# An MLP's second product on quarters by Strassen's scheme, interleaved with the next group's first product

## The chip, the core and the metric

The kernel runs on one core of one Trainium2 chip. The metric is device microseconds from start to end of one execution; the verdict on a change compares medians of several runs of both kernels.

## What is computed

One layer of a hybrid decoder, for a prompt of 1024 tokens and a sample of 8 x 8 = 64 tokens that share the weights (`D_MODEL` 1024, `D_FF` 4096). After the mixer and its output projection comes the part that the change touches:

```python
    x = x + gate1[:, None] * mixed

    h2 = rms_norm(x, norm2_g[l]) * (1.0 + scale2[:, None]) + shift2[:, None]
    ff = jnp.square(jax.nn.relu(h2 @ w_ff1[l])) @ w_ff2[l]
    x = x + gate2[:, None] * ff
```

The gate is one vector for the whole prompt, and another for each of the eight samples.

## The kernel before

Features lie on the partitions, tokens on the free axis: 1088 tokens in three chunks `CH` of 384, 384 and 320, the last with 256 prompt and the 64 sample tokens. Inputs are fp32. Every operand of a large product is kept as two fp32r parts, `hi` (a rounded copy, made by ACT) and `lo` (the remainder, made by a subtraction on DVE or POOL), and a product is three matmuls: hi x hi, hi x lo, lo x hi (`product`, whose matmuls all stand at line 150 of the profile).

`x1` (128 x 8 x 1088) holds x after the output projection (`out_block`), and `h2` the normed and modulated parts (`make_h2`). The 4096 hidden features go in `NG` = 8 groups of 4 blocks of 128. `ff1(g)` is the first product of a group: for 4 blocks and 3 chunks a product over 8 blocks of `h2` (24 matmuls), then relu (L1270) and square (L1272) on ACT, and DVE squares again in fp32 and subtracts to get the low part (L1273, L1274). `ff2(g)` is the second: for 8 output blocks and 3 chunks a product over the group's 4 blocks (12 matmuls), which DVE multiplies by the gate and adds into `x1` (`add_gated`, L1180 for the prompt, L1183 and L1185 for the sample). `ff1(g + 1)` is issued ahead of `ff2(g)`, so that TensorE always has a whole product between a group's hidden features and their use.

Weights come as 512 KB tiles over SP's queue (two raw tiles `w`), ACT copies `wh` (L229), POOL forms `wl` in the MLP and DVE before it (L230). Products go round four PSUM banks `mm`. TensorE keeps the order in which the code is written; on ACT, DVE, POOL and SP a scheduler sets the order from the dependencies, and each then runs its queue in order. In the last group every output block is stored as it is finished.

## Time and profile before

| | us |
|---|---|
| median of 3 runs (1263.47 to 1264.85) | 1263.8 |
| the profiled execution | 1262.94 |
| its span, first to last instruction | 1261.1 |
| TensorE busy (7836 matmuls) | 1243.6 |
| DVE busy | 657.1 |
| ACT busy | 375.7 |
| POOL busy | 173.6 |

Busy time counts an engine's instructions, not what they achieve: matmuls overlap in TensorE's pipeline, so that one has a length of about 0.33 us while the next starts after 0.15 to 0.17. The distance of starts is what a matmul costs. The granted clock of TensorE was full (2.4 GHz) in 0.999 of the span.

### The profile page before, as it was taken

How to read it: one execution, taken by the hardware profiler on the slowest of the kernel's cores; microseconds unless marked ns; L12 is line 12 of the kernel's file. 1: busy time of each engine (PE TensorE's matmuls, PEld its weight loads, DVE VectorE, ACT ScalarE, POOL GpSimd, SP SyncE). 2: the span in 40 equal slices, each digit the busy share in tenths (PEclk: the TensorE clock that was granted, in tenths of full speed). 3: DMA queues.
4: the chain of work that ended last, by engine and by line, in shares of the span. 5: the costliest groups of instructions: out<-in, count | busy, mean ns of one | idle time of the engine just before them, and what ended most of it. 6: DMA issues, size and time to landing. Idle time of an engine off the chain costs nothing.

```text
span 1261.1 us, 18691 instructions
## 1 busy us (share of the span) xinstructions
PE 1243.6 (99%) x7836; PEld 1194.4 (95%) x7836; DVE 657.1 (52%) x1272; ACT 375.7 (30%) x724; POOL 173.6 (14%) x103
## 2 busy tenths in 40 slices
PE   8899999999999999999999999999999999999998
PEld 6698789998899999999999999999999999999998
DVE  4789798894786539644334334334334334334333
ACT  5372333432465316533023123023023023023000
POOL 3300000000000000022212112112122122122120
PEclk9999999999999999999999999999999999999999
DMA  9548811120122601011111111111111111110122
GB/s 363 187 131 310 219 51 51 51 53 19 35 70 79 197 18 35 1 51 50 35 50 50 34 51 46 39 50 43 42 51 41 45 50 38 46 51 34 50 78 99
DMA packets 41067, 94.42 MB, mean 75 GB/s; under 512 B 11799, under 2 KB 21143, under 8 KB 40983
## 3 DMA queue, kind: packets, MB, share of 16 engines
q1 hardware_dynamic: 40839, 93.16, 23.1%
q8 instruction: 61, 1.00, 0.3%
q14 instruction: 23, 0.19, 0.0%
q10 hardware_dynamic: 144, 0.07, 0.0%
HBM read 86.70 MB, written 6.52 MB: 74 GB/s over the span
## 4 chain that ended last, share of the span: by engine, by line
PE 92%; DVE 4%; DMA 2%; ACT 1%; issue 0%; SPq 0%; DVEq 0%
PE mm L150 85%; PE pm L150 5%; PE pm L154 1%; PE ada L150 1%; DMA ada<-in_ada 1%; DVE ut L279 1%; DMA M<-in_xT 1%; DMA glu<-in_st_conf 0%; DVE lo L286 0%; DVE M L588 0%; DVE lo L283 0%; DVE sq L421 0%; DVE sq L419 0%; DVE uhi L1205 0%; ACT hi L453 0%
## 5 line engine op out<-in xcount | busy, mean ns | idle before, releaser
L150 PE MATMUL mm<-hi,wh 128*128 128x384 f32 (+1 forms) x1208 | 397.9, 329 | 0.1
L150 PE MATMUL mm<-lo,wh 128*128 128x384 f32 (+1 forms) x1208 | 394.4, 327 | 2.1 <-DVE lo L455 2.0
L150 PE MATMUL mm<-hi,wl 128*128 128x384 f32 (+1 forms) x1208 | 394.2, 327 | 0.5 <-DVE wl L230 0.5
L230 POOL TENSOR_TENSOR wl<-w,wh 128x1024 fp32r<-128x1024 f32 x61 | 146.8, 2406 | 843.8 <-ACT wh L229 843.8
L1180 DVE SCALAR_TENSOR_TENSOR x<-mm,mod,x 128x384 f32<-128x384 f32 (+1 forms) x216 | 123.6, 572 | 253.0 <-PE mm L150 244.5
L150 PE MATMUL mm<-uhi,wl 128*128 128x384 f32 (+1 forms) x768 | 251.3, 327 | 0.0
L150 PE MATMUL mm<-ulo,wh 128*128 128x384 f32 (+1 forms) x768 | 250.9, 327 | 0.0
L150 PE MATMUL mm<-uhi,wh 128*128 128x384 f32 (+1 forms) x768 | 250.8, 327 | 0.0
L150 PEld LDWEIGHTS mm<-hi,wh 128*128 128x128 f32 x1208 | 226.9, 188 | 7.7 <-issue 6.0
L150 PEld LDWEIGHTS mm<-lo,wh 128*128 128x128 f32 x1208 | 227.0, 188 | 2.9 <-DVE lo L455 2.9
L150 PEld LDWEIGHTS mm<-hi,wl 128*128 128x128 f32 x1208 | 226.9, 188 | 0.8 <-DVE wl L230 0.8
L1273 DVE TENSOR_TENSOR ut<-ut 128x384 f32<-128x384 f32 (+1 forms) x96 | 95.0, 991 | 237.0 <-ACT uhi L1272 237.0
L229 ACT CAST wh<-w 128x1024 fp32r<-128x1024 f32 x83 | 87.0, 1048 | 433.1 <-PE mm L150 433.1
L150 PEld LDWEIGHTS mm<-uhi,wl 128*128 128x128 f32 x768 | 144.3, 188 | 0.0
L150 PEld LDWEIGHTS mm<-uhi,wh 128*128 128x128 f32 x768 | 144.2, 188 | 0.0
L150 PEld LDWEIGHTS mm<-ulo,wh 128*128 128x128 f32 x768 | 144.2, 188 | 0.0
L588 DVE SCALAR_TENSOR_TENSOR M<-glu,cmix,M 128x512 f32<-128x512 f32 (+2 forms) x150 | 97.9, 668 | 2.0
L1270 ACT ACTIVATE ut<-mm 128x384 f32<-128x384 f32 (+1 forms) x96 | 45.1, 471 | 174.4 <-PE mm L150 174.4
L1274 DVE TENSOR_TENSOR ulo<-ut,uhi 128x384 fp32r<-128x384 f32 (+1 forms) x96 | 51.2, 534 | 3.1
L1272 ACT ACTIVATE uhi<-ut 128x384 fp32r<-128x384 f32 (+1 forms) x96 | 48.7, 509 | 2.9
L150 PE MATMUL mm<-hi,ulo 128*128 128x384 f32 (+1 forms) x144 | 47.0, 326 | 0.0
L150 PE MATMUL mm<-lo,uhi 128*128 128x384 f32 (+1 forms) x144 | 47.0, 326 | 0.0
(229 smaller groups left out, 1125.2 us busy)
## 6 DMA issues: line engine op xcount, KB each, us to landing
w<-in_w_ff SPq DMA_DIRECT2D x64, 512.0 KB, 3.6
w<-in_w_in SPq DMA_DIRECT2D x22, 512.0 KB, 5.1
M<-in_ada SPq DMA_DIRECT2D x20, 512.0 KB, 4.6
ada<-in_ada SPq DMA_DIRECT2D x16, 512.0 KB, 10.2
sw<-in_ada SPq DMA_DIRECT2D x9, 512.0 KB, 5.0
w<-in_w_out SPq DMA_DIRECT2D x8, 512.0 KB, 3.6
out_yT<-x SPq DMA_DIRECT2D x7, 544.0 KB, 2.7
M<-in_xT SPq DMA_DIRECT2D x2, 1536.0 KB, 11.0
```

The source lines that it names most:

```text
L150: return tc.keep_in_program_order(nc.tensor.matmul(*args, **kw))
L154: return tc.keep_in_program_order(nc.tensor.transpose(*args, **kw))
L229: ACT.copy(hi, raw)
L230: lo_engine.tensor_tensor(out=lo, in0=raw, in1=hi, op=ALU.subtract)
L279: DVE.scalar_tensor_tensor(t[:, :w], src[:, :w], a[:, k, 0:1], r[:, :w], ALU.mult, ALU.mult)
L588: DVE.scalar_tensor_tensor(dst, src(t), cdw[:, j, t : t + 1], dst, ALU.mult, ALU.add))))
L1180: DVE.scalar_tensor_tensor(dst[:, :pw], ps[:, :pw], gate[:, 0:1], dst[:, :pw], ALU.mult, ALU.add)
L1270: ACT.activation(t, ps, AF.Relu)
L1272: ACT.activation(uh, t, AF.Square)
L1273: DVE.tensor_tensor(out=t, in0=t, in1=t, op=ALU.mult)
L1274: DVE.tensor_tensor(out=ul, in0=t, in1=uh, op=ALU.subtract)
```

## The change

The seven groups 0 to 6 run their second product by Strassen's scheme in Winograd's form. The group's weights (4 x 8 blocks) and its hidden prompt features (4 blocks x 1024 tokens) are each cut in four quarters: `quarter(g, i, j)` loads a quarter of the weights (i the half of the output features, j the half of the group's hidden blocks) as one 512 KB tile, and `u.quarter(i, j)` is a tile of 128 x 1024 hidden features. In place of eight quarter products there are seven, on quarters or on sums of quarters: DVE adds or subtracts whole fp32 quarters (`s` of weights, `t` of features), `form` has ACT copy the high part (`ah`, `qh`) and DVE subtract the low part (`al`, `ql`), and `products` runs 6 matmuls of 512 columns for each of 4 output blocks. Each result is added into one or two quarters of `x1` (`add_to`), 40 additions in a group.

`x1` therefore holds the sums of the scheme and not x any more: x is stored to a DRAM tensor `x1_save` after the output projection, read back at the end (`xr`), and the gate is applied once, after the last group. The last group runs its eight quarter products straight, on top of the sums.

The 64 sample tokens take no part in the scheme. Their features, high and low part side by side (`st`, 128 columns), are the stationary operand and the unsummed weight quarters the moving one: 4 quarters x 4 matmuls of 512 columns a group, added in `acc`; at the end `pair` adds the two halves (4 fp32 matmuls of 64 columns for each half of the outputs).

The work is written as seven `slot`s a group, with one or two products of the next group's first part between (`ff1_items`, 12 in a group). DVE forms all low parts, POOL has none. ACT and DVE, from group 0's first product on, keep the order in which the code is written (`InOrder`). Hidden features stay fp32 until a slot needs their parts. Seven PSUM banks go round, the eighth is the sample's. The tiles' rooms change with it (`room`), `ut` takes `qh` and `ql` in turn.

```diff
-    ACT, DVE, POOL = nc.scalar, nc.vector, nc.gpsimd
+    POOL = nc.gpsimd
+    pinned = [False]
+    class InOrder:
+        def __init__(self, engine):
+            self.engine = engine
+        def __getattr__(self, name):
+            f = getattr(self.engine, name)
+            if not pinned[0] or name.startswith("dma"):
+                return f
+            def kept(*args, **kw):
+                i = f(*args, **kw)
+                tc.keep_in_program_order(i)
+                return i
+            return kept
+    ACT, DVE = InOrder(nc.scalar), InOrder(nc.vector)
...
+        BUFS = {"ar": 2, "ah": 2, "al": 2, "qh": 2, "ql": 2, "q12": 2}
+        def room(tag, dtype=F32):
+            if tag[0] == "w":
+                return wp.tile([P, 1024], dtype, tag=tag, name=nm(tag), bufs=2)
+            return up.tile([P, 1024], dtype, tag=tag, name=nm(tag), bufs=BUFS.get(tag, 1))
...
-            return up.tile([P, 384], dtype, tag="ut", name=nm("ut"), bufs=5)[:, :w]
+            UT.append(UT.pop(0))
+            return room(UT[-1], dtype)[:, :w]
...
+        def cast(raw, hi, lo):
+            ACT.copy(hi, raw)
+            return lambda: DVE.tensor_tensor(out=lo, in0=raw, in1=hi, op=ALU.subtract)
+        def two(raw, hi_tag, lo_tag):
+            hi, lo = room(hi_tag, F32R), room(lo_tag, F32R)
+            cast(raw, hi, lo)()
+            return hi, lo
...
+        RAW = ("w", "w", "ar", "ar")
+        turn["raw"] = 0
+        def quarter(g, i, j):
+            raw = room(RAW[turn["raw"] % 4])
+            turn["raw"] += 1
+            nc.sync.dma_start(raw.rearrange("p (q f) -> p q f", q=2),
+                              A["w_ff2"][g, 2 * i : 2 * i + 2].rearrange("q p f -> p q f")[:, :, H * j : H * j + H])
+            return raw
+        def block(w, k, m):
+            s = (m // 2) * H + k * 256 + (m % 2) * P
+            return w[:, s : s + P]
+        def products(ps, m, w, u, start, stop):
+            for k in range(2):
+                uh, ul = (x[:, k * H : k * H + H] for x in u)
+                wh, wl = (block(x, k, m) for x in w)
+                PE.matmul(ps, wh, uh, start=start and k == 0, stop=False)
+                PE.matmul(ps, wh, ul, start=False, stop=False)
+                PE.matmul(ps, wl, uh, start=False, stop=stop and k == 1)
...
+        def ff1_split(x, hi="wh", lo="wl"):
+            if x < NG * G:
+                ff1_weights[x] = two(ff1_weights[x], hi, lo)
+        def ff1_block(u, x, c, ps):
+            product(ps, *ff1_weights[x], act_of(h2, c), range(8))
+        def ff1_out(u, x, c, ps):
+            for cols, dst in u.pieces(x % G, c):
+                ACT.activation(dst, ps[:, cols], AF.Relu)
+                ACT.activation(dst, dst, AF.Square)
...
+        save = nc.dram_tensor("x1_save", (P, 8, SEQ), F32, kind="Internal").ap()
+        nc.sync.dma_start(save, x1[:, :, 0:SEQ])
+        pinned[0] = True
+        acc = wide_room("acc")
+        BANKS = [f"mm{x}" for x in range(4)] + [f"pm{x}" for x in range(3)]
+        def next_bank():
+            BANKS.append(BANKS.pop(0))
+            return pp.tile([P, 512], F32, tag=BANKS[-1], name=nm("ps"))
...
+        def form(raw, side):
+            parts = room(side + "h", F32R), room(side + "l", F32R)
+            return parts, cast(raw, *parts)
...
+            if first and g == 0:
+                if minus:
+                    DVE.tensor_scalar_mul(dst, ps, -1.0)
+                else:
+                    DVE.tensor_copy(dst, ps)
+            else:
+                DVE.tensor_tensor(out=dst, in0=dst, in1=ps, op=ALU.subtract if minus else ALU.add)
...
+            st = up.tile([P, G, P], F32R, tag="st", name=nm("st"), bufs=1)
+            ACT.copy(st[:, :, 0:64], u.sample)
+            DVE.tensor_tensor(out=st[:, :, 64:P], in0=u.sample, in1=st[:, :, 0:64], op=ALU.subtract)
+            return st
+        def sample_product(ps, st, w, j, start, stop):
+            for k in range(2):
+                for x in range(2):
+                    PE.matmul(ps.rearrange("p (q m) -> p q m", q=2), st[:, 2 * j + k, :],
+                              w[x].rearrange("p (q k m) -> p q k m", q=2, k=2)[:, :, k, :],
+                              start=start and k == x == 0, stop=stop and k == x == 1)
...
-        def ff2(g, u, last):
-            for mp in range(4):
-                hi, lo = weight_split(*weight(A["w_ff2"][g, mp], POOL))
-                for m2 in range(2):
-                    m = 2 * mp + m2
-                    for c, (c0, w) in enumerate(CH):
-                        ps = mm_psum(w)
-                        product(ps, hi, lo, lambda k: (u[c][0][:, k, :], u[c][1][:, k, :]), range(G),
-                                lambda x: (2 * x + m2) * P)
-                        add_gated(x1[:, m, c0 : c0 + w], ps, c, mod[:, 40 + m, :], ut() if c == 2 else None)
-                        if last and m == 7:
-                            nc.sync.dma_start(O["yT"][:, m, c0 : c0 + w], x1[:, m, c0 : c0 + w])
-                    if last and m < 7:
-                        nc.sync.dma_start(O["yT"][:, m], x1[:, m])
-        u = ff1(0)
-        for g in range(NG):
-            nxt = ff1(g + 1) if g + 1 < NG else None
-            ff2(g, u, g == NG - 1)
-            u = nxt
...
+        def first_parts(g, u, a11):
+            t = room("t")
+            DVE.tensor_tensor(out=t, in0=u.quarter(0, 1), in1=u.quarter(0, 0), op=sub)
+            w, r0 = form(a11, "a")
+            v, r1 = form(u.quarter(0, 0), "q")
+            r0()
+            r1()
+            return t, (w, v)
+        a11 = quarter(0, 0, 0)
+        t, now_parts = first_parts(0, u, a11)
+        s = quarter(0, 1, 0)
+        a22, a12 = quarter(0, 1, 1), quarter(0, 0, 1)
...
+                    ps = next_bank()[:, : CH[c][1]]
+                    ff1_block(nu, x, c, ps)
+                    ff1_out(nu, x, c, ps)
+                    if c == 0:
+                        ff1_split(x + 1)
+                        ff1_load(x + 2)
...
+            def slot(parts, targets, rests):
+                rests = list(rests)
+                for m in range(4):
+                    ps = next_bank()
+                    products(ps, m, *parts, True, True)
+                    if rests:
+                        rests.pop(0)()
+                    for i, j, minus, first in targets:
+                        add_to(g, (i, j, m, minus, first), ps)
...
+            DVE.tensor_tensor(out=s, in0=s, in1=a22, op=add)
+            w, r0 = form(s, "a")
+            v, r1 = form(t, "q")
+            parts2 = (w, v)
+            slot(now_parts, [(0, 0, 0, 1), (1, 1, 0, 1)], [r0, r1])
+            st = sample_parts(g, u)
+            ff1_items(1)
+            sm = sample_bank()
+            sample_product(sm, st, now_parts[0], 0, True, False)
+            ff1_items(1)
+            DVE.tensor_tensor(out=s, in0=s, in1=a11, op=sub)
+            DVE.tensor_tensor(out=t, in0=u.quarter(1, 1), in1=t, op=sub)
+            w, r0 = form(s, "a")
+            v, r1 = form(t, "q")
+            parts3 = (w, v)
...
+            w, r0 = form(a21, "a")
+            slot(parts7, [(1, 0, 0, 0)], [r0])
+            sm = sample_bank()
+            sample_product(sm, st, parts7[0], 1, True, False)
+            sample_product(sm, st, w, 0, False, True)
+            sample_out(g, 1, sm)
+            if not last:
+                a11 = nxt
+                t, now_parts = first_parts(g + 1, nu, a11)
+                a22, a12 = quarter(g + 1, 1, 1), quarter(g + 1, 0, 1)
+            else:
+                weights, parts = {(0, 0): two(nxt, "ah", "al")}, {(0, 0): two(nu.quarter(0, 0), "qh", "ql")}
+            ff1_items(1)
+            u = nu
...
+        weights[0, 1] = two(s, "ah", "al")
+        for ij, tags in (((1, 0), ("qh", "ql")), ((0, 1), ("q12", "t")), ((1, 1), ("fr", "q11"))):
+            parts[ij] = two(u.quarter(*ij), *tags)
+        st = sample_parts(g, u)
+        for j in range(2):
+            weights[1, j] = two(quarter(g, 1, j), "wh", "wl")
+        xr = [hp.tile([P, 4, CH[0][1]], F32, tag=("hi0", "lo0", "hi1", "lo1")[m % 4], name=nm("xr")) for m in range(8)]
+        xr = [x.rearrange("p a b -> p (a b)")[:, 0:SEQ] for x in xr]
+        for m in range(8):
+            nc.sync.dma_start(xr[m], save[:, m, :])
+        s22 = x1[:, 4:8, H:SEQ]
+        for x in (x1[:, 0:4, H:SEQ], x1[:, 4:8, 0:H]):
+            DVE.tensor_tensor(out=x, in0=x, in1=s22, op=ALU.add)
...
+        for i in range(2):
+            sm = sample_bank()
+            for j in range(2):
+                sample_product(sm, st, weights[i, j], j, j == 0, j == 1)
+            sample_out(g, i, sm)
+            for t in range(2):
+                for m in range(4):
+                    ps = next_bank()
+                    for j in range(2):
+                        products(ps, m, weights[i, j], parts[j, t], j == 0, j == 1)
+                    x = x1[:, 4 * i + m, H * t : H * t + H]
+                    gate = mod[:, 40 + 4 * i + m, 0:1]
+                    DVE.scalar_tensor_tensor(x, x, gate, xr[4 * i + m][:, H * t : H * t + H], ALU.mult, ALU.add)
+                    DVE.scalar_tensor_tensor(x, ps, gate, x, ALU.mult, ALU.add)
+                    if t == 0 and m == 1:
+                        sample_end(i)
+                    nc.sync.dma_start(O["yT"][:, 4 * i + m, H * t : H * t + H], x)
```

Where the scheme starts, ACT's queue was, at the end of group 0's first product (`mm` 741 is its last block, 752 the first of group 1):

```order
L1270 ACTIVATE ut_740_5291<-mm_739_5266 128x320 [waits DVE_49,PE_49]
L1272 ACTIVATE uhi2_690_4883<-ut_740_5291 128x320 [waits Activation_49]
L1270 ACTIVATE ut_742_5321<-mm_741_5296 128x320 [waits DVE_49,PE_49]
L1272 ACTIVATE uhi2_690_4883<-ut_742_5321 128x320 [waits Activation_49]
L1270 ACTIVATE ut_753_5363<-mm_752_5338 128x384 [waits DVE_49,PE_49]
L1272 ACTIVATE uhi0_743_5326<-ut_753_5363 128x384 [waits Activation_49]
L1270 ACTIVATE ut_755_5393<-mm_754_5368 128x384 [waits DVE_49,PE_49]
L1272 ACTIVATE uhi1_745_5328<-ut_755_5393 128x384 [waits Activation_49]
L229 CAST wh_768_5526<-w_767_5524 128x1024 [waits DMAHW6_49,PE_49,Pool_49]
```

and is now (`mm` 730 is that last block, `q22` and `us` its prompt and sample part, `w` the quarter (0, 0), `q11` the features' quarter):

```order
L1359 ACTIVATE q22_724_5155<-mm_730_5277 128x256 [waits PE_49]
L1359 ACTIVATE us_727_5214<-mm_730_5277 128x64
L1360 ACTIVATE q22_724_5155<-q22_724_5155 128x256 [waits Activation_49]
L1360 ACTIVATE us_727_5214<-us_727_5214 128x64 [waits Activation_49]
L158 CAST wh_733_5310<-fr_731_5306 128x1024 [waits DMAHW7_49]
L158 CAST ah_738_5320<-w_736_5316 128x1024 [waits DMAHW5_49]
L158 CAST qh_740_5323<-q11_700_4929 128x1024
L158 CAST ah_745_5335<-w_742_5328 128x1024 [waits DMAHW6_49,DVE_49]
L158 CAST qh_747_5338<-t_737_5318 128x1024
```

Before, the next block of the first product followed at once; now the copies of the first quarter stand there.

At a group's end DVE's queue was (group 0's second product: two output blocks of three chunks; nothing else stood between):

```order
L1180 SCALAR_TENSOR_TENSOR x1_3993<-mm_792_5767,mod_76,x1_3993 128x384 [waits PE_49]
L1180 SCALAR_TENSOR_TENSOR x1_3993<-mm_793_5781,mod_76,x1_3993 128x384 [waits PE_49]
L1180 SCALAR_TENSOR_TENSOR x1_3993<-mm_794_5795,mod_76,x1_3993 128x256 [waits PE_49]
L1183 TENSOR_TENSOR ut_795_5808<-mm_794_5795,mod_76 128x64
L1185 TENSOR_TENSOR x1_3993<-ut_795_5808,x1_3993 128x64 [waits DVE_49]
L1180 SCALAR_TENSOR_TENSOR x1_3993<-mm_799_5818,mod_76,x1_3993 128x384 [waits PE_49]
L1180 SCALAR_TENSOR_TENSOR x1_3993<-mm_800_5832,mod_76,x1_3993 128x384 [waits PE_49]
```

and is now, from the last slot of group 1 to the first additions of group 2 (`sm` the sample's product, `t`, `al` and `ql` the next group's first parts, `ar` 920 its `s`, `ps` 945 its first product):

```order
L158 TENSOR_TENSOR x1_3993<-x1_3993,ps_931_6695 128x512 [waits PE_49]
L158 TENSOR_TENSOR acc_732_5309<-sm_932_6703,acc_732_5309 128x512 [waits PE_49]
L158 TENSOR_TENSOR t_933_6713<-q12_859_6157,q11_853_6118 128x1024 [waits DVE_49]
L158 TENSOR_TENSOR al_935_6716<-ar_908_6498,ah_934_6715 128x1024 [waits DMAHW2_49,Activation_49]
L158 TENSOR_TENSOR ql_937_6719<-q11_853_6118,qh_936_6718 128x1024 [waits Activation_49]
L158 TENSOR_TENSOR ar_920_6603<-ar_920_6603,w_938_6723 128x1024 [waits DMAHW6_49,DMAHW5_49]
L158 TENSOR_TENSOR al_942_6758<-ar_920_6603,ah_941_6757 128x1024 [waits Activation_49]
L158 TENSOR_TENSOR x1_3993<-x1_3993,ps_945_6763 128x512 [waits PE_49]
L158 TENSOR_TENSOR x1_3993<-x1_3993,ps_945_6763 128x512
L158 TENSOR_TENSOR ql_944_6761<-t_933_6713,qh_943_6760 128x1024 [waits Activation_49]
```

The parts for the next slot now stand behind the sample's sum, and the additions behind `al` of the slot after it.

In the last group ACT only copied weights, one tile ahead:

```order
L229 CAST wh_1335_10650<-w_1334_10648 128x1024 [waits DMAHW3_49,PE_49,Pool_49]
L229 CAST wh_1346_10746<-w_1345_10744 128x1024 [waits DMAHW4_49,PE_49,Pool_49]
L229 CAST wh_1357_10844<-w_1356_10842 128x1024 [waits DMAHW5_49,PE_49,Pool_49]
L229 CAST wh_1368_10942<-w_1367_10940 128x1024 [waits DMAHW6_49,PE_49,Pool_49]
L229 CAST wh_1379_11040<-w_1378_11038 128x1024 [waits DMAHW7_49,PE_49,Pool_49]
```

and it now copies, behind that group's last block of hidden features (`q22`, `us`), the pieces of all its quarters and then `st`:

```order
L158 ACTIVATE q22_1399_10078<-ps_1423_10268 128x256 [waits PE_49]
L158 ACTIVATE q22_1399_10078<-q22_1399_10078 128x256 [waits Activation_49]
L158 ACTIVATE us_1360_9790<-ps_1423_10268 128x64
L158 ACTIVATE us_1360_9790<-us_1360_9790 128x64 [waits Activation_49]
L158 CAST ah_1424_10297<-ar_1409_10156 128x1024 [waits DMAHW3_49,DVE_49]
L158 CAST qh_1426_10301<-q21_1386_10003 128x1024
L158 CAST q12_1428_10305<-q12_1349_9712 128x1024
L158 CAST fr_1430_10309<-q22_1399_10078 128x1024
L158 CAST st_1432_10313<-us_1360_9790 128x4x64 [waits Activation_49]
L158 CAST wh_1434_10318<-ar_1433_10316 128x1024 [waits DMAHW4_49]
```

The sample's product, the first of the group on TensorE, needs `st`.

## Rows read from the trace of the kernel before

**Rows 1.** Busy table of the page, and the chain's last piece (start, length, matmuls)

```profile
PE 1243.6 (99%) x7836; PEld 1194.4 (95%) x7836; DVE 657.1 (52%) x1272; ACT 375.7 (30%) x724; POOL 173.6 (14%) x103
...
505.66 751.29 PE mm L150 x4560
```

**Rows 2.** Timeline, TensorE in one second product: start, length, instruction

```profile
902.02 0.33 PE L150 MATMUL mm<-uhi,wl 128*128 128x384 f32 x1
...
904.62 0.34 PE L150 MATMUL mm<-uhi,wl 128*128 128x384 f32 x1
...
905.08 0.31 PE L150 MATMUL mm<-uhi,wl 128*128 128x320 f32 x1
...
906.40 0.31 PE L150 MATMUL mm<-uhi,wl 128*128 128x320 f32 x1
```

**Rows 3.** Last group's first and second product by engine (busy, instructions), PEclk, DMA

```profile
1161.90:1209.30 47.40, 47.40 (x289) 47.40 (x289) 17.94 (x39) 4.93 (x6) 9.56 (x4) 1.00 0.13 45
1209.30:1256.70 47.40, 47.40 (x289) 47.37 (x287) 16.62 (x40) 3.14 (x3) 7.17 (x3) 1.00 0.26 98
```

**Rows 4.** DVE: timeline of independent operations back to back; groups by form (mean ns)

```profile
61.56 1.22 DVE L230 TENSOR_TENSOR ak<-w,ak 128x1024 fp32r<-128x1024 f32 x1
62.70 0.17 DVE L401 SCALAR_TENSOR_TENSOR a<-mod,cfirst 128x18 f32<-128x18 f32 x1
...
515.11 0.68 DVE L292 TENSOR_TENSOR uhi<-uhi,a 128x512 f32<-128x512 f32 x1
515.71 0.55 DVE L1273 TENSOR_TENSOR ut<-ut 128x384 f32<-128x384 f32 x1
...
L1148 DVE TENSOR_TENSOR M<-mm,M 128x384 f32<-128x384 f32 x4 | 2.2, 557 | 0.4 <-PE mm L150 0.4
```

**Rows 5.** ACT: timeline of a copy and its successor; groups by form

```profile
24.48 1.03 ACT L229 CAST wh<-w 128x1024 fp32r<-128x1024 f32 x1
25.41 0.71 ACT L453 ACTIVATE hi<-M,mod,a 128x384 fp32r<-128x384 f32 x1
...
L1272 ACT ACTIVATE uhi<-ut 128x384 fp32r<-128x384 f32 x64 | 33.6, 526 | 1.9
L1270 ACT ACTIVATE ut<-mm 128x384 f32<-128x384 f32 x64 | 31.3, 490 | 170.0 <-PE mm L150 170.0
L1272 ACT ACTIVATE uhi<-ut 128x320 fp32r<-128x320 f32 x32 | 15.1, 473 | 1.0
...
L1270 ACT ACTIVATE ut<-mm 128x320 f32<-128x320 f32 x32 | 13.8, 432 | 4.4 <-PE mm L150 4.4
```

**Rows 6.** TensorE's long idle times early on, and stretches (length, PE busy, PEclk)

```profile
38.00 0.88 PE L150 MATMUL pm<-sq,ones 128*128 128x384 f32 x2 [2.87 <-DVE sq L421]
48.25 0.44 PE L150 MATMUL pm<-lo,wh 128*128 128x384 f32 x1 [3.12 <-DVE lo L455]
...
35.00:45.00 10.00, 7.05 (x62) 1.00 1.07 359
45.00:49.80 4.80, 1.68 (x8) 1.00 0.11 15
49.80:53.40 3.60, 3.60 (x14) 0.53 0.00 0
```

**Rows 7.** Timeline: eight matmuls with `pair`

```profile
21.72 1.00 PE L150 MATMUL pm<-pair,tmp 128*128 128x64 f32 x8
```

**Rows 8.** DMA issues: count, size, median us from issue to landing

```profile
w<-in_w_ff SPq DMA_DIRECT2D x64, 512.0 KB, 3.6
...
ada<-in_ada SPq DMA_DIRECT2D x16, 512.0 KB, 10.2
...
out_yT<-x SPq DMA_DIRECT2D x7, 544.0 KB, 2.7
```

**Rows 9.** Timeline: the last matmul and what follows it

```profile
1256.62 0.31 PE L150 MATMUL mm<-uhi,wl 128*128 128x320 f32 x1
1256.97 0.48 DVE L1180 SCALAR_TENSOR_TENSOR x<-mm,mod,x 128x256 f32<-128x256 f32 x1 [1.13 <-PE mm L150]
...
1257.62 0.22 DVE L1185 TENSOR_TENSOR x<-ut,x 128x64 f32<-128x64 f32 x1
```

151 lines of the change are left out of this document (116 added, 35 removed).

## The prediction

> **What bounds the kernel now.** I read the busy table and the chain first. TensorE is busy for 1243.6 of 1261.1 us, and the chain ends in one unbroken piece of 4560 matmuls, 751.29 us long, from 505.66 us to the end [rows 1]: the whole MLP. In the last group's two stretches, 47.4 us each, TensorE is busy in all of it, DVE in 16.6 to 17.9 us, and ACT and POOL in under 10 [rows 3]. So only fewer or cheaper matmuls shorten this part, and any new wait on TensorE lengthens it by its full length.
>
> Then the price of a matmul. Fifteen starts at 384 columns lie 2.60 us apart (902.02 to 904.62), 0.1733 each; nine at 320 columns take 1.32 us (905.08 to 906.40), 0.1467 each [rows 2]. The difference of 64 columns costs 26.7 ns, 0.417 ns a column, which leaves 13.3 ns in each matmul that does not depend on its columns. One product (a stretch of rows 3) is 96 x (2 x 0.1733 + 0.1467) = 47.36 us, as the stretches show. At 512 columns I take 0.2133 + 0.0133 = 0.2267 us.
>
> **What TensorE saves.** The second product of a group was 288 matmuls, 47.36 us. Now seven quarter products of 4 blocks x 6 matmuls make 168, and the sample's four quarters 16 more: 184 x 0.2267 = 41.71 us. That is 5.65 less, and 39.5 us in the seven groups that run so. The eighth group keeps eight quarter products: (192 + 16) x 0.2267 = 47.15, 0.2 less, plus eight fp32 matmuls with `pair`, 1.00 us as eight of them took earlier [rows 7]. TensorE's own sum is **-38.8 us**. The first product is the same 288 matmuls in both.
>
> By the Trainium skill's page "TensorE: Matmul & The Clock Gate" (section "Wait — 56ns, not 53.3ns?") the constant is about 2.5 ns, not 13.3. The rows show 13.3 for these fp32r pairs at two widths, so the sum keeps it; the page's figure is taken up under the rivals.
>
> **What the other engines now do.** Start to start, an independent 1024-wide DVE subtraction takes 1.14 us (result after 1.22), a 512-wide one 0.60 (result after 0.68), and a PSUM source does not change it (0.557 at 384, against 0.55 from SBUF) [rows 4]. A 1024-wide ACT copy takes 0.93 us start to start, 1.03 to its result [rows 5]. A group asks of DVE 40 additions of 512 into `x1` (24 us), 15 low parts, 8 quarter sums and 4 weight splits of 1024 (27 x 1.14 = 30.8 us) and about 2 us for the sample: 57 us in a group of some 90. ACT copies 19 x 0.93 and does the relus and squares, about 32 us. POOL has nothing left. No engine is near full; the question is order, since ACT and DVE are now pinned.
>
> Call T0 the moment when TensorE has issued the last matmul of a group's seventh quarter product. I walked the three queues through a group with these prices.
>
> *Group boundary.* TensorE goes on with 8 sample matmuls (1.81 us) and one 320-wide block of the next first product (24 x 0.1467 = 3.52) and reaches the next group's first quarter at T0 + 5.33. DVE can add the sample's sum only when those 8 are done, at T0 + 2.0 (DVE starts 0.35 us after the start of a last matmul [rows 9]). Behind it stand `t`, the weight's low part and `ql`: starts at 2.60, 3.74 and 4.88, `ql` done at 6.10. The second matmul needs `ql` and would have started at 5.56: **0.6 us** of waiting.
>
> *Sample parts.* DVE then forms `s` (done 7.24), waits for ACT's copy of it (8.33), and does `al`, two additions, `ql`, six additions and only then the low half of `st`, done at about 15.9. TensorE, 6.15 + 23 x 0.2267 + 24 x 0.1733, wants `st` at 15.5: **0.4 us**.
>
> In the later slots each pair of parts is ready 3 us or more before TensorE gets there, though DVE waits there for ACT, which stands behind a block's relu. A group is so 41.71 + 47.36 + 1.0 = 90.1 us, against 94.7. Six such boundaries: **+6.0 us**.
>
> *Start of the scheme.* Before, TensorE went from group 0's first product to group 1's. Now nothing is interleaved there. The last block (320 wide) leaves TensorE; ACT starts 0.2 us after, does two relus and two squares (0.49 and 0.526 at 384, 0.432 and 0.473 at 320 [rows 5], so about 1.15 us for 256 and 64 columns), then three copies; `qh` is there after 4.2 us. DVE does `wl` from 2.4, `t`, `al`, `ql`: done at 7.06. TensorE issues one matmul in between, so it idles **6.9 us**.
>
> *Last group.* At T0 + 5.33 TensorE has nothing without `st`, which stands behind ACT's last block (to 6.7), copies of four raw pieces and of `st` (to 10.8), and DVE's low parts, one from 7.75, then four more at 1.14 each, `st` at 12.73. That is **7.4 us**.
>
> *The clock.* After 3.12 us without a matmul (to 48.25) the granted clock was half (mean 0.53) over 49.8 to 53.4 us; an idle 2.87 us before 38.00 left it full [rows 6]. Both long waits should so be followed by one such stretch, which loses 0.47 x 3.6 = **1.7 us each**; the short ones should not. In group 0 the slower start covers the 0.4 us of `st`.
>
> *What I cost at nothing.* Writing `x1` out (4 MB, some 21 us at the rate of 544 KB in 2.7 [rows 8]) lies under group 0's first product of 47 us; uncovered it would hold back the first copies into `x1`. Reading it back starts about 10 us before T0 and shares SP's queue with the quarter for `weights[1, 0]`. If these loads run one by one at 3.6 us [rows 8], that quarter lands some 8 us after ACT wants it and `sample_end` stops TensorE for up to 6 us; with several in flight I take 0 and keep 6 for the range. The out-projection in front runs the same matmuls with four scratch tiles in place of five, and had no wait there: 0. At the end two DVE operations of 384 in all (1256.97 to 1257.84 [rows 9]) become one of 512 and a 256 KB store: +0.2.
>
> **Sum:** -38.8 + 6.0 + 6.9 + 1.7 + 7.4 + 1.7 + 0.2 = -14.9 us. From the profiled execution, 1262.94 us, this gives 1248.0; the median of the runs is 0.86 above that execution, so I forecast **1249 us** (-1.2%). The bounds of the single terms: if DVE's operations do not overlap at all, each addition costs 0.08 more, 8 to 10 of them before `st`, and each low part as much: 1.3 us a group, 8 in all; without any half clock 3.4 less, with twice as much 3.4 more. The forecast's own range is 1243 to 1257.
>
> **The rivals.**
>
> *Cheaper wide matmuls.* If the constant does not carry over to 512 columns, 1496 matmuls (7 x 184 + 208) lose 13.3 ns less the remainder. For it: only two widths were measured, and whatever the constant is may hide behind a longer matmul. Against: it was the same at both. With nothing left of it the bound is 1496 x 13.3 ns = 20 us, 1229. By the 2.5 ns of the Trainium skill's page "TensorE: Matmul & The Clock Gate" it would be 16 us, 1233. Chance 0.11.
>
> *DVE without overlap, or clock losses twice as long*, singly or together: 1254 to 1260. For it: two additions of one product read the same bank, which no row shows. Chance 0.16.
>
> *Late quarters, which ends slower.* The next group's second weight quarter can load only when the tile of a quarter of this group is free, after DVE's `al` of `a21` at about T0 - 1.6, and DVE wants it at T0 + 6.0: 7.6 us. It then blocks DVE's queue, with `s`, `al`, all eight additions, `st` and so TensorE behind it, one for one. Against: w loads land 3.6 us after issue in this part. For: 512 KB took 10.2 us in the busy part [rows 8], and a quarter now comes in pieces of half the length. At 10.2 us it costs 2.6 us in each of six groups and the result is 1264.6, the time of before; it decides from there, and at 12 us it gives 1275. Chance 0.08.
>
> *Short waits that drop the clock, also slower.* If waits of 0.4 to 0.6 us cost a half-clock stretch, twelve of them lose 20 us: 1269. Against: TensorE waited 2.87 us at full clock. Chance 0.05.
>
> *It does not do what it says:* the walk misses a dependency in the pinned queues, and DVE falls behind by a slot. Slack is 3 to 5 us in each slot; the gain of 15 us is gone when 2.1 us are lost in each group. 1257 to 1275, chance 0.10.
>
> **How the numbers follow.** The forecast keeps 0.50. For this kernel 0.2% (2.5 us, below 1261.3 or above 1266.3) is about what can be told from no change. Faster: 0.50 + 0.11 + 0.16, and a little of the missed dependency: 0.78, of which I take 0.02 back for the unknown: 0.76. Within 0.2%: a third each of the last and of the late quarters, 0.08. Slower: the rest, 0.16. The range 1236 to 1266 leaves out most of the cheap matmuls and the upper ends of the three slower cases, together about 0.2.
>
> **What would show it.** Right: starts 0.227 us apart at 512 columns; 90.1 us from a group to the next; per group two TensorE waits for DVE, on `ql` and on `st`, of 0.6 and 0.4 us; one wait of some 7 us after group 0's first product and one before the last group, each followed by about 3.5 us of half clock; POOL idle in the MLP; DVE busy for two thirds of a group. Wrong: starts 0.216 us apart; a TensorE or DVE wait on a DMA at group boundaries; granted clock below 1 in the middle of groups; waits on `ql` in slots 2 to 7.

## The result, and the profile after

The changed kernel takes 1250.45 us (median of 4 runs, 1249.12 to 1252.66) against 1264.01 of the kernel before beside it. The ratio is 0.9894, with a 95% interval of 0.9877 to 0.9911. So it is 1.1% faster, where 1249 (1.2%) was forecast. The profiled execution is 1249.56 us long; 1248.0 was worked out for it.

The page of the changed kernel: busy time by engine, the granted clock in 40 slices, and pieces of the chain, which is the work that ended last, followed back step by step: the two long ones of a group and the first of the next (start, length, matmuls). PEld are TensorE's weight loads.

```profile
PE 1215.0 (97%) x7044; PEld 1099.9 (88%) x7044; DVE 819.2 (66%) x1297; ACT 469.8 (38%) x943; POOL 30.0 (2%) x43
...
PEclk9899999999999999989999999999999999999989
...
835.33 35.97 PE ps L171 x192
872.21 36.66 PE ps L171 x192
...
925.85 35.97 PE ps L171 x192
```

Against [rows 1] there are 792 fewer matmuls on TensorE. Its busy time falls by 28.6 us and the span only by 13.3 (1261.1 to 1247.8): the difference is new idle time. The chain shows it as well. Before, the MLP was one piece; now the same pieces come back every 90.52 us (835.33 to 925.85), where 90.1 was forecast. The two slices with an 8 in the granted clock behind the first lie at the start of the scheme and before the last group, where half clock was forecast; the first 8 is in front of the MLP.

What TensorE waited for in the MLP (in all, times, longest, in us):

```profile
PE sm L171 <- DVE st L158: 7.8, 4, 7.3
PE ps L171 <- DVE ql L158: 4.4, 7, 2.0
PE ps L171 <- ACT qh L158: 3.9, 1, 3.9
```

These are the tiles that were named: `qh` and `ql` once at the start of the scheme, `ql` at each of the six group boundaries, `st` once before the last group. (Idle time is counted here from the modelled end of the matmul in front, so a wait of 0.3 us is nearly or wholly lost; `st` therefore appears 4 times, not 7.) The three places in TensorE's timeline (start, length, instruction, idle time before it): start of the scheme, a group boundary with its later wait on `st`, last group.

```profile
549.03 0.79 PE L171 MATMUL ps<-qh,ah 128*128 128x512 f32 x1 [3.90 <-ACT qh L158]
551.81 0.80 PE L171 MATMUL ps<-ql,ah 128*128 128x512 f32 x1 [1.98 <-DVE ql L158]
552.40 0.63 PE L171 MATMUL ps<-qh,al 128*128 128x512 f32 x1
552.83 0.63 PE L171 MATMUL ps<-qh,ah 128*128 128x512 f32 x1
...
732.98 0.40 PE L171 MATMUL ps<-qh,ah 128*128 128x512 f32 x1
733.82 0.50 PE L171 MATMUL ps<-ql,ah 128*128 128x512 f32 x1 [0.44 <-DVE ql L158]
...
743.18 0.34 PE L171 MATMUL ps<-hi,wl 128*128 128x384 f32 x1
743.64 0.47 PE L171 MATMUL sm<-ah,st 128*128 128x512 f32 x1
...
1193.13 0.77 PE L171 MATMUL sm<-ah,st 128*128 128x512 f32 x1 [7.35 <-DVE st L158]
```

A wait is best read as the distance of two starts less the price of the matmul between them. At the boundary 733.82 - 732.98 - 0.227 = 0.61 us; on `st` 743.64 - 743.18 - 0.173 = 0.29. At the start of the scheme the two gaps are 4.05 and 2.55 us, in the last group 7.5 us. Behind both long waits the starts are 0.43 us apart (552.40 to 552.83): half clock, as stretches show (us, PE, PEld, DVE, ACT, POOL, granted clock, DMA):

```profile
548.23:555.05 6.82, 4.04 (x9) 2.85 (x10) 5.71 (x6) 2.88 (x4) 0.00 (x0) 0.50 0.40 105
1189.93:1196.76 6.83, 3.63 (x9) 2.90 (x10) 6.83 (x7) 3.09 (x4) 0.00 (x0) 0.50 0.01 2
...
733.00:743.00 10.00, 9.56 (x47) 8.28 (x47) 8.88 (x12) 3.48 (x7) 0.00 (x0) 1.00 0.19 52
```

The first two stretches begin inside the waits: half clock was granted for 6.8 us each time, of which the matmuls behind the wait met 3.2 (551.81 to 555.05) and 3.6 us (1193.13 to 1196.76). The third row is the stretch behind a short wait: full clock. DVE's timeline at the same boundary is the queue that the prediction had walked through:

```profile
729.67 0.69 DVE L158 TENSOR_TENSOR acc<-sm,acc 128x512 f32<-128x512 f32 x1 [1.13 <-PE sm L171]
730.27 1.22 DVE L158 TENSOR_TENSOR t<-q,q 128x1024 f32<-128x1024 f32 x1
731.41 1.22 DVE L158 TENSOR_TENSOR al<-ar,ah 128x1024 fp32r<-128x1024 f32 x1
732.54 1.22 DVE L158 TENSOR_TENSOR ql<-q,qh 128x1024 fp32r<-128x1024 f32 x1
...
739.49 3.68 DVE L158 TENSOR_TENSOR x<-x,ps 128x512 f32<-128x512 f32 x6
```

DVE stands 1.13 us for the sample's product, and only then does `t`, the low part of the weight and `ql`. Six additions take 3.68 us, (3.68 - 0.68) / 5 = 0.60 from one to the next, as in [rows 4].

### The profile page after: what moved, and what is told of

The parts are those of the page before. It is cut to its first block, busy times and chain, and to the rows that moved or that the text cites. A ratio compares the mean times of both kernels' runs of the same rounds, so it can differ in the third digit from the quotient of the medians.

```text
span 1247.8 us, 17276 instructions
## 1 busy us (share of the span) xinstructions
PE 1215.0 (97%) x7044; PEld 1099.9 (88%) x7044; DVE 819.2 (66%) x1297; ACT 469.8 (38%) x943; POOL 30.0 (2%) x43
## 4 chain that ended last, share of the span: by engine, by line
PE 87%; DVE 9%; DMA 2%; ACT 1%; issue 1%; SPq 0%; DVEq 0%
PE ps L171 48%; PE mm L171 29%; PE pm L171 5%; PE sm L171 3%; DVE x L158 1%; PE pm L175 1%; PE ada L171 1%; DVE al L158 1%; DVE ql L158 1%; DMA ada<-in_ada 1%; DMA M<-in_xT 1%; DMA glu<-in_st_conf 0%; ACT ah L158 0%; DVE qh L301 0%; DVE lo L308 0%
## 5 line engine op out<-in xcount | busy, mean ns | idle before, releaser
L171 PE MATMUL ps<-hi,wl 128*128 128x384 f32 (+1 forms) x672 | 219.4, 326 | 0.0
L171 PE MATMUL ps<-hi,wh 128*128 128x384 f32 (+1 forms) x672 | 219.2, 326 | 0.0
L171 PE MATMUL ps<-lo,wh 128*128 128x384 f32 (+1 forms) x672 | 219.0, 326 | 0.0
L171 PE MATMUL mm<-hi,wh 128*128 128x384 f32 (+1 forms) x536 | 178.4, 333 | 0.1
L171 PE MATMUL mm<-lo,wh 128*128 128x384 f32 (+1 forms) x536 | 174.8, 326 | 2.0 <-DVE lo L476 2.0
L171 PE MATMUL mm<-hi,wl 128*128 128x384 f32 (+1 forms) x536 | 174.4, 326 | 0.5 <-DVE wl L252 0.5
L158 DVE TENSOR_TENSOR x<-x,ps 128x512 f32<-128x512 f32 x264 | 165.9, 682 | 1.0
L171 PE MATMUL ps<-ql,ah 128*128 128x512 f32 x408 | 160.9, 394 | 4.4 <-DVE ql L158 4.4
L171 PE MATMUL ps<-qh,ah 128*128 128x512 f32 x408 | 159.9, 392 | 3.9 <-ACT qh L158 3.9
L171 PE MATMUL ps<-qh,al 128*128 128x512 f32 x408 | 160.0, 392 | 0.0
```

The source lines that it names most:

```text
L158: i = f(*args, **kw)
L171: return tc.keep_in_program_order(nc.tensor.matmul(*args, **kw))
```

## The experiments

The part in front of the MLP does the same work in every kernel here but its length is not quite the same: TensorE starts the MLP's third block at 505.0 to 507.4 us in the profiled executions. Where a median is hard to read I therefore also give the MLP alone, from that matmul to the end of the span (its first two blocks, 48 matmuls, run before the norm is finished and are left out in every kernel alike). It is 755.6 us in the kernel before (505.49 to 1261.1) and 741.9 in the changed one (505.94 to 1247.8).

| kernel | median, us (lowest to highest) | ratio to before, 95% interval | MLP, us |
|---|---|---|---|
| changed kernel | 1250.45 (1249.12 to 1252.66) | 0.9894 (0.9877 to 0.9911) | 741.9 |
| fillers 28 and 50 | 1251.15 (1250.56 to 1252.89) | 0.9901 (0.9886 to 0.9916) | 743.0 |
| fillers 28 and 33 | 1247.62 (1246.30 to 1248.76) | 0.9869 (0.9855 to 0.9884) | 739.2 |
| eighth product | 1288.56 (1286.98 to 1290.88) | 1.0196 (1.0181 to 1.0212) | 781.2 |
| x1 not through DRAM | 1250.88 (1250.57 to 1253.06) | 0.9903 (0.9886 to 0.9919) | 741.9 |
| quarter loaded three times | 1267.77 (1264.86 to 1272.06) | 1.0032 (1.0019 to 1.0044) | 759.7 |
| sample's sum later | 1245.95 (1245.59 to 1247.62) | 0.9860 (0.9846 to 0.9875) | 738.2 |
| the same, `st` early | 1243.82 (1242.63 to 1244.71) | 0.9836 (0.9821 to 0.9850) | 735.4 |
| start reordered | 1245.53 (1244.85 to 1247.43) | 0.9856 (0.9841 to 0.9870) | 738.1 |
| last group reordered | 1245.36 (1244.21 to 1245.99) | 0.9851 (0.9836 to 0.9865) | 737.0 |
| ACT and DVE not pinned | 1236.11 (1234.44 to 1237.03) | 0.9778 (0.9761 to 0.9794) | 726.4 |
| not pinned, last group reordered | 1227.70 (1227.32 to 1228.12) | 0.9714 (0.9697 to 0.9730) | 718.3 |
| all edits, pinned | 1226.67 (1225.98 to 1227.27) | 0.9700 (0.9686 to 0.9715) | 718.1 |

**Is the MLP still bound by TensorE, and what does a matmul of 512 columns cost?**

```diff
             slot(parts7, [(1, 0, 0, 0)], [r0])
+            for m in range(4):
+                products(next_bank(), m, *parts7, True, True)
```

> Edit: in each of the seven groups the last quarter product is computed a second time into four banks that nobody adds (24 matmuls of 512 columns more, as many as an eighth quarter product would have; no work for DVE or ACT). My theory: TensorE sets the time and a matmul of 512 columns costs 0.2267 us, so 7 x 24 x 0.2267 = 38.1 us more, less the 1.1 us waits at six boundaries, which now find DVE with 5.4 us more: 1282 to 1288.5. Rival A, the group is bound by DVE's or ACT's order and TensorE has slack: clearly less than 30 us more, under 1280. Rival B, cheap wide matmuls (0.216): 36.3 more at most, 1280 to 1286.8, told from the theory by the starts in the trace.

It took 1288.56, 38.1 us more than the changed kernel: full price, so there was no slack under TensorE. In the chain of this kernel the piece of a group that holds the extra product has grown from the 36.66 us and 192 matmuls above to:

```profile
794.41 42.10 PE ps L171 x216
...
890.40 42.10 PE ps L171 x216
```

5.44 us for 24 matmuls, 0.2267 each; cheap wide matmuls are out. One part of the expectation was wrong: the waits on `ql` did not go. `ql` still comes 0.60 us late (the group takes 95.99 us from 794.41 to 890.40, 90.52 + 5.47), because DVE's sum waits for the sample's product on TensorE, and this was moved by the same 5.44 us. The wait hangs from TensorE's own position, not from how busy DVE is.

**Is it the half clock that costs time behind the long waits?** Fillers keep TensorE at work while it waits.

```diff
+        def fill(n):
+            spare = sample_bank()
+            for _ in range(n):
+                PE.matmul(spare[:, 0:P], ones, ones, start=True, stop=True)
+
+        fill(28)
         for g in range(NG - 1):
...
+        fill(50)
         for i in range(2):
             sm = sample_bank()
```

> Edit: 28 small matmuls (128 columns, on the constant tile `ones`, into a spare bank nobody reads) before the first slot of the scheme, 50 more before the last group's sample product; nothing else changes. The changed kernel waits there 6.6 us (4.05 + 2.55) and 7.5 us, and runs at half clock after each, which costs about 1.6 us each time. My theory: the half clock comes from the idle stretch, so the two stretches go back to full clock, the waits for DVE and ACT stay as long, and the time falls by 3.2 us, from 1250.45 to about 1247.2 (starts 0.227 us apart right behind both waits in place of 0.425). Rival A, the half clock comes for another reason (the new kind of work, the load): it stays, and the time is 1250 to 1251. Rival B, the fillers delay the work behind them: 1251 or more.

1251.15: rival B by the time, but for a reason that belongs to the experiment. The 50 fillers were too many: they ran for 11.3 us, 0.226 each, in a gap of 7.5 us. The second kernel has 33 in their place.

```diff
-        fill(50)
+        fill(33)
```

> Edit: as the first filler kernel, 28 fillers before the first slot, but 33 in place of 50 before the last group's sample product, since one took 0.226 us there and the wait is 7.5 us. My theory: no half clock behind either wait; the first place gains 1.1 us as it did in the first filler kernel (1.6 us of half clock, less the 0.4 us of waiting on `st` that the slower start had covered), the last one 1.6: 1250.45 - 2.7 = about 1247.7. Rival, the half clock was not what cost the time: 1250 or more.

1247.62, 2.8 less than the changed kernel, as expected. Its timeline (a filler counts as two instructions):

```profile
546.01 6.41 PE L171 MATMUL sm<-ones 128*128 128x128 f32 x56
...
552.84 0.49 PE L171 MATMUL ps<-ql,ah 128*128 128x512 f32 x1 [0.18 <-DVE ql L158]
553.17 0.39 PE L171 MATMUL ps<-qh,al 128*128 128x512 f32 x1
553.40 0.40 PE L171 MATMUL ps<-qh,ah 128*128 128x512 f32 x1
...
1185.59 7.53 PE L171 MATMUL sm<-ones 128*128 128x128 f32 x66
1193.17 0.50 PE L171 MATMUL sm<-ah,st 128*128 128x512 f32 x1
```

The needed matmuls come no earlier after the last product than before, but behind them the starts are 0.23 apart in place of 0.43. So the stretches at half clock follow the idle time. Without them the MLP is 2.7 us shorter, and that is net of a wait of 0.28 us on `st` in group 0, which the slower start had covered.

**Does the way of `x1` through DRAM cost anything?**

```diff
-        save = nc.dram_tensor("x1_save", (P, 8, SEQ), F32, kind="Internal").ap()
-        nc.sync.dma_start(save, x1[:, :, 0:SEQ])
...
-        for m in range(8):
-            nc.sync.dma_start(xr[m], save[:, m, :])
+        nc.sync.dma_start(xr[0], A["xT"][:, 0, 0:SEQ])
```

> Leaves out: x1 is not written to DRAM, and at the end one 512 KB piece of the input is read in place of the eight pieces of x1 (the residual of the output is therefore that of another tensor). My theory: saving and reloading 4 MB each way lies under TensorE's work and costs nothing: 1250 to 1251 (within 0.5 us of 1250.45). Rival, the store holds back group 0's first copies or the reload holds back the last group's weights: up to 6 us less, down to 1244.5.

1250.88, and the MLP takes the same 741.9 us. 8 MB of transfers lie under TensorE's work entirely.

**How much room do the weight quarters have?** The quarter that DVE adds first at a boundary is loaded three times over.

```diff
-                a22, a12 = quarter(g + 1, 1, 1), quarter(g + 1, 0, 1)
+                a22, a12 = quarter(g + 1, 1, 1, 3), quarter(g + 1, 0, 1)
```

> Edit: at each of the six boundaries between the groups of the scheme the weight quarter that DVE adds first (`a22`) is loaded three times, one load after the other into the same tile; nothing else changes. One such load took 3.5 us from issue to landing in the changed kernel, so the third lands some 10.5 to 11 us after the first is issued. My theory, the rival of late quarters in the prediction: the slack is 7.6 us, DVE waits 3 to 3.4 us more at each boundary, with all its queue and so TensorE behind it one for one, less nothing: 6 x 3 to 3.4 = 18 to 20 us, 1268.5 to 1271, with waits of TensorE on `st` of 3.5 us. Rival, the slack is larger than I counted or the parts of the later slots make up for it: under 1256.

1267.77, 17.3 more, which is near the number and not by the way that I had put down. The wait appears at three of the six boundaries. TensorE at a boundary that waits, then DVE's sum there:

```profile
653.86 0.34 PE L171 MATMUL ps<-hi,wl 128*128 128x384 f32 x1
657.71 0.47 PE L171 MATMUL sm<-ah,st 128*128 128x512 f32 x1 [3.52 <-DVE st L158]
```

```profile
647.74 1.23 DVE L158 TENSOR_TENSOR w<-w,w 128x1024 f32<-128x1024 f32 x1 [3.30 <-DMA w<-in_w_ff]
```

Seven quarters a group go in turn through two pairs of tiles. At every other boundary the tile of this quarter had been free for long, and its three loads were issued at 718 to 725 us, well before DVE's sum at 739.86. At the three others the room is what the prediction counted: in the changed kernel that load was issued at 635.58 and wanted at 643.15, 7.57 us. The three gaps there are 3.68, 5.12 and 3.45 us in place of 0.3 each, together 11.4; behind each TensorE runs at half clock, and that makes up the rest of the 17.8 us by which the MLP is longer (6.4; by the distances of starts 1.7, 2.2 and 2.9 us). The dearest of the three, from the end of its wait on:

```profile
1031.52:1037.56 6.04, 6.04 (x18) 5.65 (x19) 3.27 (x3) 0.00 (x0) 0.00 (x0) 0.50 0.55 173
```

The mechanism is shown, with half the places and the clock's loss on top.

**What sets the waits at a boundary?** First the sample's sum goes behind the first parts, then `st` also goes forward.

```diff
-            sample_out(g, 1, sm)
             if not last:
                 a11 = nxt
                 t, now_parts = first_parts(g + 1, nu, a11)
...
+            sample_out(g, 1, sm)
             ff1_items(1)
```

> Edit: the sum of the sample's last product into its accumulator is issued on DVE behind the next group's first parts (`t`, low part of the weight, `ql`) in place of in front of them; nothing else changes. My theory: at a group boundary DVE is late by what stands behind that sum (it must wait for the sample product itself), so TensorE's wait on `ql` (0.61 and 0.1 of refill) and on `st` (0.3 and 0.08) both go, 1.1 us in each of six boundaries: from 1250.45 to about 1243.8, period of a group 89.4 in place of 90.5. Rival, ACT's copies are what comes late and the sum only hides it: the waits stay or move to ACT, 1249.5 to 1250.5. A mix (the first wait goes, the second stays) would give 1246.

1245.95, the mix: no wait on `ql` at the boundaries any more, but `st` comes 0.39 us late in all six, and the period is 89.92 us (743.98 to 833.90 in its chain). DVE has the same work ahead of `st`, whatever its order.

```diff
             DVE.tensor_tensor(out=s, in0=s, in1=a22, op=add)
+            st = sample_parts(g, u)
             w, r0 = form(s, "a")
...
             slot(now_parts, [(0, 0, 0, 1), (1, 1, 0, 1)], [r0, r1])
-            st = sample_parts(g, u)
```

> Edit: the sample's last sum stands behind the next group's first parts, as before, and in addition the sample's parts `st` are formed right behind the first weight sum of a group in place of behind the eight additions of its first slot. That kernel without the second edit gave 1245.95, with a wait of 0.39 us on `st` in six groups and none on `ql`. My theory: this wait is DVE's queue up to `st` and nothing else; formed 12 operations earlier it is there in time, 6 x 0.39 = 2.3 us less, 1243.6, period 89.5 us in place of 89.9. Rival, DVE stands in `st`'s new place for ACT's copy and all behind it comes later: 1245.5 or more, with the wait on another part (`ql` or `al` of the second slot).

1243.82. The wait on `st` at the boundaries is gone too. The chain of this kernel, two pieces a group apart:

```profile
833.80 35.97 PE ps L171 x192
...
923.24 35.97 PE ps L171 x192
```

89.44 us is what TensorE alone needs for a group; the six waits of 1.1 us were DVE's written order and nothing else.

**The start.** Blocks 2, 3, 0, 1 in the last third of group 0's first product, with the first parts formed beside them:

```diff
-        t, now_parts = first_parts(0, u, a11)
+        w, r0 = form(a11, "a")
+        v, r1 = form(u.quarter(0, 0), "q")
+        r0()
+        r1()
+        now_parts = w, v
+        ff1_first(2, 3)
+        ff1_first(2, 0)
...
+        ff1_first(2, 1)
+        t = room("t")
```

> Edit: the last third of group 0's first product runs its blocks in the order 2, 3, 0, 1, and the first quarter's parts (`ah`, `al`, `qh`, `ql`) are formed beside the blocks 3 and 0, `t` behind block 1; the work is the same. My theory: the wait of 6.6 us at the start of the scheme is the chain relu, square, three copies, four low parts behind the last block; with the parts formed earlier it goes, and the 1.6 us of half clock behind it too, but the 0.4 us waits of group 0 on `st` that the slow start covered appear: 1250.45 - 7.8 = about 1242.6. Rival A, only a part is hidden, and TensorE waits as long one slot later for the second pair of parts: 1246 to 1250. Rival B, the pinned queue makes the relus late and stops TensorE inside the first product: 1250 or more.

1245.53: nearest to rival A, 0.5 us below its range and by another wait than it names. The 6.6 us are gone, and a new wait stands some 10 us behind the scheme's first matmul, with half clock behind it. TensorE's timeline, then the stretch (columns as above):

```profile
556.13 0.50 PE L171 MATMUL sm<-ah,st 128*128 128x512 f32 x1 [2.20 <-DVE st L158]
...
558.13 0.53 PE L171 MATMUL ps<-lo,wh 128*128 128x384 f32 x1
558.45 0.53 PE L171 MATMUL ps<-hi,wl 128*128 128x384 f32 x1
```

```profile
557.40:561.00 3.60, 3.60 (x14) 3.60 (x13) 2.08 (x2) 0.00 (x0) 0.00 (x0) 0.53 0.70 215
```

It is `st` again, behind eight copies into `x1` on DVE. I had looked at the second pair of parts and not at `st`.

**The last group.**

```diff
...
+                if first:
+                    for m in range(4):
+                        products(banks[m], m, weights[i, 0], parts[0, t], True, False)
                 for m in range(4):
+                    if first:
+                        ps = banks[m]
+                        products(ps, m, weights[i, 1], parts[1, t], False, True)
...
-                    if t == 0 and m == 1:
+                    if t == 1 and m == 1:
                         sample_end(i)
...
+                if t == 0:
+                    sm = sample_bank()
...
```

> Edit: the last group starts with the products of weights[0, 0] into four banks, goes on with weights[0, 1] into the same banks, and only then does the sample's product; `sample_end` comes half a product later. The work is the same. My theory: TensorE stood 7.5 us for `st` with both parts of weights[0, 0] ready; now `st` has 10.9 us (48 matmuls of 0.2267) more, so the wait and the 1.6 us of half clock behind it go: 1250.45 - 9.1 = about 1241.3. Rival, weights[0, 1] and its part of `u` come as late as `st` (they stand in the same queues ahead of it): the first 24 matmuls cover 5.4 us and some 2 us of wait are left, 1243 to 1245.

1245.36: neither of the two cases. The wait of 7.5 us and its half clock are gone, and the rival's 2 us on weights[0, 1] did not come. But TensorE stops a product later, at `sample_end`. TensorE and DVE there:

```profile
1204.96 0.39 PE L171 MATMUL ps<-fr,al 128*128 128x512 f32 x1
1207.79 1.42 PE L171 MATMUL ps<-pair,acc 128*128 128x64 f32 x8 [2.44 <-DVE acc L158]
```

```profile
1196.59 4.48 DVE L158 TENSOR_TENSOR x<-x 128x2048 f32<-128x2048 f32 x2
...
1207.05 0.68 DVE L158 TENSOR_TENSOR acc<-sm,acc 128x512 f32<-128x512 f32 x1
```

DVE is behind by then: two sums of 2048 columns and the outputs of the first product stand in front of the accumulator. 2.6 us of waiting and 1.5 us of half clock took nearly half of the gain back.

**The written order itself.** ACT and DVE are pinned to the order of the program text in the scheme. This kernel leaves them to the scheduler.

```diff
-        pinned[0] = True
```

> Edit: from the second product on ACT and DVE are no longer held to the order in which the program is written; the scheduler orders them as it does in the rest of the kernel. TensorE's order stays. My theory has two sides: the waits at the boundaries come from the written order of DVE (the sample's sum ahead of the first parts), so a scheduler that takes what is ready first gains up to 6.6 us, 1244; but one that does not know which part TensorE waits for puts additions ahead of low parts, and at 2 to 4 operations of 0.6 to 1.1 us in seven slots per group this costs more: 1255 to 1290. I expect the second.

1236.11: the side that I did not expect, and more than its bound. DVE at a boundary of this kernel:

```profile
720.49 1.23 DVE L1258 TENSOR_TENSOR ql<-t,qh 128x1024 fp32r<-128x1024 f32 x1 [0.40 <-ACT qh L1257]
721.63 0.68 DVE L1421 TENSOR_TENSOR acc<-sm,acc 128x512 f32<-128x512 f32 x1
722.23 2.35 DVE L1258 TENSOR_TENSOR al<-ar,ah 128x1024 fp32r<-128x1024 f32 x2
...
726.89 4.87 DVE L1400 TENSOR_TENSOR x<-x,ps 128x512 f32<-128x512 f32 x8
```

The scheduler has `ql` done ahead of the sample's sum, and all low parts ahead of the additions: it does what the hand edits above do, and at the start as well. The group takes 89.44 us, the start of the scheme has no gap over 0.11 us, and of the waits only the last group's is left (5.8 us), where TensorE's own order asks for `st` first. Two kernels follow from this: the scheduler's order with the last group rewritten, and all edits by hand. In both `sample_end` of the first half comes a product later than in the experiment above.

```diff
-                    if t == 1 and m == 1:
-                        sample_end(i)
+                    if i == 1 and m == 1:
+                        sample_end(t)
```

> Edit: ACT and DVE are left to the scheduler again (1236.11), and the last group starts with the products of weights[0, 0], with `sample_end` of the first half one product later, as in the kernel with all edits. Theory: the written order of ACT and DVE is the only cause of the waits at the start and at the six boundaries, and the last group's wait (5.8 us in the kernel left to the scheduler, and 1.6 of half clock) comes from TensorE's own order, which the scheduler can't change: 1236.11 - 7.4 = about 1228.7. Rival, the scheduler puts the last group's parts late and a wait moves to weights[0, 1] or to the accumulator: 1231 to 1236.

> Edit: all of the single edits together (the sample's last sum behind the first parts; `st` early; the order 2, 3, 0, 1 at the start with the first parts beside it; the last group from weights[0, 0] on), with two mends: the start's remaining wait of 2.4 us was for `st`, which is early here, and `sample_end` of the first half comes one product later, since its wait of 2.6 us for the accumulator and the half clock behind it took back what the last group had gained. My theory: every wait named so far goes: 6.6 (six boundaries) + 8.2 (start) + 9.1 (last group): 1250.45 - 23.9 = about 1226.5, TensorE without a gap of over 0.5 us in the MLP and without half clock. Rival, the engines behind are now late elsewhere (DVE in the last group, second slot of group 0) and take 3 to 6 us back: 1229 to 1233.

1227.70 and 1226.67, 1.8% and 1.9% below the changed kernel. The granted clock on the page of the kernel with all edits:

```profile
PEclk9899999999999999999999999999999999999999
```

TensorE has no gap over 0.1 us from 507.4 us to its last matmul. The MLP is 23.8 us shorter than in the changed kernel; 23.9 had been added up from the single waits and the half clock behind them. What is left is TensorE's own work: 714.03 us from the start of the third block to the last matmul's start, for 751.13 in the kernel before. Against the kernel before it is 3.0% faster (ratio 0.9700, 0.9686 to 0.9715).

## Why the prediction was right, and where it was off

The forecast and its reasons held: every term of the sum can be found in the traces, the waits at the places and on the tiles that were named.

| term | forecast, us | measured, us |
|---|---|---|
| TensorE's own sum | -38.8 | -37.1 (714.03 with all edits, less 751.13) |
| of it: a group before | 94.7 | 94.96 |
| of it: a group of the scheme | 89.07 | 89.44 |
| of it: the matmuls with `pair` | 1.0 | 1.6 |
| waits at a boundary (`ql` 0.6, `st` 0.4) | 1.0 | 1.09 (90.53 - 89.44), the first 0.92 |
| wait at the start of the scheme | 6.9 | 6.6 |
| wait before the last group | 7.4 | 7.5 |
| half clock behind each | 1.7 | 1.6 and 1.8 |
| tail | +0.2 | -0.4 (last matmul's start to the end: 4.1 for 4.5) |
| `x1` through DRAM | 0 | 0.0 |

TensorE's own sum is mis-sized, by 1.7 us. The price of 512 columns is not the reason: the eighth product shows 0.2267 a matmul, as carried over from the narrower widths. What the forecast left out are the steps between widths. TensorE in the kernel with `st` early: the first and the eleventh start of a run of 24, and the first matmul behind it.

```profile
837.80 0.39 PE L171 MATMUL ps<-qh,ah 128*128 128x512 f32 x1
...
840.11 0.39 PE L171 MATMUL ps<-ql,ah 128*128 128x512 f32 x1
...
843.28 0.30 PE L171 MATMUL ps<-hi,wh 128*128 128x320 f32 x1
```

The first ten starts behind the narrower matmuls take 2.31 us, 0.231 each, the next fourteen 3.17, 0.226 each. Such steps up in width cost 0.02 to 0.04 us each; over a group of the scheme they make the 0.37 us. The kernel before has them too, which the product of 47.36 us missed: the place of 902.02 [rows 2] comes back 94.96 us later, not 94.72.

```profile
996.98 0.33 PE L150 MATMUL mm<-uhi,wl 128*128 128x384 f32 x1
```

So a group saves 5.52 and not 5.65, about 0.9 us in seven. The other part is `pair`: an fp32 matmul shows as two instructions, so that the row of eight in [rows 7] is four matmuls, as many as one half of the outputs needs. Each half takes 0.81 us here from its start to the next product's:

```profile
1201.62 1.00 PE L171 MATMUL ps<-pair,acc 128*128 128x64 f32 x8
```

In the MLP alone 740.7 was forecast (755.6 - 14.9) and 741.9 measured: 1.7 more of TensorE's own work and 0.4 more at the boundaries, less 0.3 at the start and 0.6 at the tail. 0.45 us more in front of the MLP make up the rest of the 1.6 us between 1248.0 and 1249.56. The errors went in both directions, and the sum gained by that.

The half clock came out right partly by luck. The forecast took one stretch of 3.6 us, all of it spent on matmuls. Half clock was granted for 6.8 us each time, and about half of that passed inside the wait. In the kernel with three loads one wait ended only 0.8 us into such a stretch, and the rest of it cost 2.9 us.

Two smaller slips change nothing in the forecast: the chain's piece of 4560 matmuls is not the whole MLP (48 more stand in front of it), and a third each of 0.10 and 0.08 is 0.06, not 0.08.

By the Trainium skill's page "TensorE: Matmul & The Clock Gate" (section "Wait — 56ns, not 53.3ns?") the constant is some 2.5 ns; an estimate from it makes the MLP 16 us shorter. The eighth product shows 13.4 ns at 512 columns (226.7 less 213.3), so the measurement decides against it here.

The rivals, point by point. *Cheap matmuls* fell with the eighth product (0.2267 each). *DVE without overlap* fell with the six additions 0.60 us apart. *Short waits that drop the clock* fell: granted clock 1.00 behind 0.6 us. *A missed dependency* did not show: no wait on `ql` in slots 2 to 7. *Late quarters* did not occur, and the experiment shows the mechanism; but its price was wrong in two ways. It exists at three boundaries of six, since I took the alternate tile to be as late as the first, and a wait of some 3.5 us also costs half clock, which the 1264.6 left out.

What the prediction took as given was the order. It walked the pinned queues and priced their waits right, but it did not ask what they would cost unpinned: 14.3 us by the medians. The expectation of that run shows the same blind spot, a scheduler that would do worse than the text.

Two expectations were wrong in a way that teaches the same thing. At the start and in the last group an edit that removed the known wait uncovered the next one in DVE's queue (`st`, then the accumulator), and I had checked the operand that TensorE needs next but not those that it needs some 10 and 18 us after the product it starts with.

## What to carry over

When an edit makes TensorE need other operands, list each operand that it will ask for in the next tens of us together with what stands in front of it in the producing engine's queue; the waits that this gives can be priced to some tenths of a us, and a wait moved away often uncovers the next one in the same queue. An order pinned by hand is a choice to be measured against the scheduler's, since here one line was worth more than the change itself. A wait of a few us on TensorE is to be priced with the half clock behind it.
